# Two-layer hybrid transformer on one core: four conditioning chunks placed right behind a branch, norm diagonals made ahead of it, and the last combine moved

## The chip, the cores and the metric

One Trainium2 chip, one of its cores. The metric is the device time of one launch in microseconds (us); lower is better. Everything runs in one program on one core: TensorE (PE) multiplies, VectorE (DVE) and ScalarE (ACT) do the elementwise work, SyncE (SP) issues nearly all loads, GpSimd (POOL) only gathers rows.

## The reference, cut to what matters

```python
def trunk_layer(x, xc, mod, mod_c, ...):
    sh1, sc1, g1, sh2, sc2, g2 = jnp.split(mod[:, None, :], 6, axis=-1)
    h = modulate(rms_norm(x, norm1), sh1, sc1)
    hc = modulate(rms_norm(xc, norm1), sh1c, sc1c)
    y, yc = token_mixer(h, hc, ...)          # attention, Fourier, pooling branches
    x = x + g1 * y
    x = x + g2 * moe_ffn(modulate(rms_norm(x, norm2), sh2, sc2), ...)
    ...
for l in range(DEPTH):                       # DEPTH = 2
    mod = jax.nn.silu(c) @ w_ada[l] + b_ada[l]        # six vectors of 1024
    mod_c = jax.nn.silu(c_ctx) @ w_ada[l] + b_ada[l]
    x, xc = trunk_layer(x, xc, mod, mod_c, ...)
return rms_norm(x, norm_f)
```

256 tokens of x and 256 context tokens, width 1024, float32. `moe_ffn` sends each token to 2 of 16 experts (1024 to 512 to 1024). In layer 2 the context is needed only as keys and values, so the mixer's outputs and the experts work on the 256 tokens of x alone.

## The kernel before, in words

The tokens stay in SBUF as four tiles of 128 rows, two in X0 and two in X1. All weights are streamed from memory once, in chunks of mostly 1 MB. `Stream` (L172 and on) holds a list of chunks in the order in which the code asks for them with `W.get`. `fill` (L187) starts the next load on SP's queue (L219) as soon as the ring it belongs to has a free buffer: the `stage` ring has four buffers, and during the experts there are seven more (`ext`) and X1. A chunk of conditioning weights (`w_ada`) is used by PE as it is, in float32, and its buffer is free when PE has read it. Every other chunk is first split (`split`, L317) by ACT into a float16 high part (`whi`, L319) and by DVE into a low part (`wlo`, L323), and each product is three float16 matmuls, high by high, high by low, low by high (`mm3`, L577, with its matmuls on L580 to L582). `W.tick` splits chunks a little ahead of their use.

Layer 1's experts end in a data-dependent branch (L1510, L1511): if more tokens than fit chose one expert, extra rounds run, else it is passed over, as here. Each engine's instructions behind the branch are scheduled apart from those ahead of it, and no instruction can be moved across it. Ahead of the branch `batch` (L1348) finishes layer 1's result and the reciprocal norms (`rstd`, L532; its last DVE operation is on L459). It also makes the stream of layer 2, `Wn`, and lets it fill the stage ring (`Wn.fill`), so four loads are on their way when the branch is reached.

Behind the branch layer 2 begins (`layer`, L585; `mixer`, L614). `norm_steps` (L543) makes four diagonal matrices from the reciprocal norms (DVE, L555), multiplies X by them (64 float32 matmul records, L568), which transposes and scales it, applies shift and scale on ACT (16 operations `h`, L572), and splits the result in DVE (`hH` L573, `hL` L574). Then come the products of K and V for all 512 tokens, with the weights of the first chunks of `w_in`, then Q, then attention with the Fourier branch between.

A conditioning vector is made by `ada(l, which)` (L462). For each of four chunks 8 float32 matmuls (16 records, L500) read the chunk with 32 columns of the stationary side each, four of them side by side; the sum is split into `adah` and `adal`, and a second small product (L477, L478) turns it. `SIDE1` holds the one vector of layer 2 that isn't made in layer 1, the shift before the experts, `ada(1, 3)`. It is taken step by step as filler work within layer 2's attention. It isn't needed before the second norm of layer 2.

Layer 2's experts end otherwise than layer 1's (`pe_all`). All results but those of the last two experts are gathered by POOL (`fetch`, L1399) into `yg`; `combine(t)` (L1404) adds the two rows of each token with their weights (ACT L1406, DVE L1407) and, where `gated`, multiplies by the gate and adds to X (DVE L1409, L1410). For expert 15, `hidden` (L1380) makes `sa` (ACT L1382, DVE L1383), and `down` multiplies it by w2 in float32 (`py`, L1312). `accumulate` (L1333) scatters and sums into `acc`, `add` puts that on X, and the last norm and the stores follow.

## Time and profile before

| what | us |
|---|---|
| runs | 1455.19, 1453.69, 1454.68 |
| median | 1454.68 |
| the profiled execution's own time | 1449.04 |
| its span in the trace | 1447.3 |
| PE busy | 1345.9 (93%) |
| DVE busy | 1118.3 (77%) |
| ACT busy | 952.8 (66%) |
| POOL busy | 16.5 (1%) |

The profile is of one execution, and times within it are counted from the start of its span. Its own time lies 1.7 us above the span and 5.64 us below the median of the runs. A view in order of time gives each instruction's start, its duration and, in brackets, how long its engine stood idle before it and what ended that. Rows with `xN` group N instructions that follow one another. The branch lies at 856 to 857 us, layer 2 behind it.

### The profile page before, as it was taken

The page shows a single profiled execution, that of the slowest core. Times are in us where ns is not written, and L with a number is a line of the kernel's source. Part 1 is how long each engine was busy: PE and PEld are TensorE (multiplying, and loading weights), DVE is VectorE, ACT ScalarE, POOL GpSimd, SP SyncE. Part 2 cuts the span into 40 slices and gives each one's busy share as a digit, 9 for nine tenths or more (in the row PEclk, how much of TensorE's full clock was granted, in tenths as well). Part 3 has the DMA queues.
Part 4 walks back from the last instruction along what each step waited for, and adds up shares of the span by engine and source line. Part 5 has one row for each costly group of instructions (what it writes and reads, how often), then busy time and mean ns, then how long its engine had stood idle before and what let it go on. Part 6 is the DMA issues. An engine that isn't in the chain of part 4 may idle for free. (4 is left out here: it accounts for less than half of the span.)

```text
span 1447.3 us, 33640 instructions
## 1 busy us (share of the span) xinstructions
PE 1345.9 (93%) x14151; PEld 923.4 (64%) x14151; DVE 1118.3 (77%) x2003; ACT 952.8 (66%) x1431; POOL 16.5 (1%) x16
## 2 busy tenths in 40 slices
PE   5999999999999998999999978899999989999994
PEld 3545445444444586777777746577788767777771
DVE  3888647786554557898988889878977888989995
ACT  3777535665433347889888656856855569899981
POOL 0000000000000000000000010000000000000010
PEclk9999999999999999999999999999999999999997
DMA  9559772678794336789999564783999679999981
GB/s 365 216 132 222 217 232 88 175 219 228 238 364 159 131 101 250 293 344 420 395 419 380 222 253 163 200 240 103 238 310 364 239 280 342 420 420 418 405 327 63
DMA packets 146416, 383.31 MB, mean 265 GB/s; under 512 B 91856, under 2 KB 93904, under 8 KB 108112
## 3 DMA queue, kind: packets, MB, share of 16 engines
q1 hardware_dynamic: 133136, 355.24, 69.5%
q10 hardware_dynamic: 11392, 19.56, 3.6%
q0 software_dynamic: 1728, 6.29, 1.3%
q8 instruction: 112, 1.84, 0.5%
q14 instruction: 48, 0.39, 0.1%
HBM read 344.88 MB, written 15.20 MB: 249 GB/s over the span
## 5 line engine op out<-in xcount | busy, mean ns | idle before, releaser
L323 DVE SCALAR_TENSOR_TENSOR wlo<-stage,whi 128x1024 f16<-128x1024 f32 (+1 forms) x212 | 318.5, 1522 | 104.0 <-ACT whi L319 103.6
L582 PE MATMUL mm<-hH,wlo 128*128 128x96 f16 (+2 forms) x1824 | 395.5, 260 | 1.0 <-DVE wlo L323 1.0
L580 PE MATMUL mm<-hH,whi 128*128 128x96 f16 (+2 forms) x1824 | 395.3, 260 | 0.7 <-DVE gate L992 0.7
L581 PE MATMUL mm<-hL,whi 128*128 128x96 f16 (+2 forms) x1824 | 395.3, 260 | 0.0
L319 ACT ACTIVATE whi<-stage 128x1024 f16<-128x1024 f32 (+1 forms) x212 | 269.6, 1294 | 126.3 <-PE mm L581 86.7
L582 PEld LDWEIGHTS <-wlo 128*128 128x128 f16 x3104 | 304.0, 98 | 72.7 <-DVE wlo L323 2.7
L580 PEld LDWEIGHTS <-whi 128*128 128x128 f16 x3104 | 303.9, 98 | 71.6 <-issue 3.4
L581 PEld LDWEIGHTS <-whi 128*128 128x128 f16 x3104 | 303.9, 98 | 71.2 <-issue 1.2
L323 DVE SCALAR_TENSOR_TENSOR wlo<-ext,whi 128x2048 f16<-128x2048 f32 x116 | 262.1, 2286 | 42.6 <-ACT whi L319 42.6
L319 ACT ACTIVATE whi<-ext 128x2048 f16<-128x2048 f32 x116 | 217.8, 1904 | 9.4 <-PE mm L582 7.4
L581 PE MATMUL mm<-xg,whi 128*128 128x96 f16 x1024 | 132.3, 206 | 0.0
L582 PE MATMUL mm<-xg,wlo 128*128 128x96 f16 x1024 | 132.3, 206 | 0.0
L580 PE MATMUL mm<-xg,whi 128*128 128x96 f16 x1024 | 132.3, 206 | 0.0
L581 PE MATMUL py<-wlo,hd 128*96 128x512 f16 x240 | 90.9, 379 | 8.9 <-DVE wlo L323 8.7
L582 PE MATMUL py<-whi,hd 128*96 128x512 f16 x240 | 90.2, 381 | 6.8 <-DVE hd L321 6.0
L580 PE MATMUL py<-whi,hd 128*96 128x512 f16 x240 | 91.0, 379 | 0.0
L580 PE MATMUL mm<-brH,whi 128*128 128x512 f16 (+1 forms) x256 | 83.5, 326 | 0.0
L582 PE MATMUL mm<-brH,wlo 128*128 128x512 f16 (+1 forms) x256 | 83.4, 326 | 0.0
L581 PE MATMUL mm<-brL,whi 128*128 128x512 f16 (+1 forms) x256 | 83.4, 326 | 0.0
L1264 PE MATMUL mm<-Dg,merged 128*128 128x384 f16 x384 | 71.0, 338 | 3.8 <-DVE Dg L1197 1.8
L500 PE MATMUL mm<-stage,cpad 128*32 128x256 f32 x768 | 58.1, 406 | 13.3 <-DMA stage<-in_w_ada_dram 13.2
L825 DVE SCALAR_TENSOR_TENSOR P<-E,rl,P 128x512 f16<-128x512 f32 (+1 forms) x96 | 59.2, 658 | 9.7 <-ACT P L824 9.5
(313 smaller groups left out, 2050.3 us busy)
## 6 DMA issues: line engine op xcount, KB each, us to landing
ext<-in_w_dram SPq DMA_DIRECT2D x118, 1024.0 KB, 9.0
stage<-in_w_dram SPq DMA_DIRECT2D x62, 1024.0 KB, 9.0
stage<-in_w_ada_dram SPq DMA_DIRECT2D x48, 1024.0 KB, 6.3
stage<-in_w_gate_dram SPq DMA_DIRECT2D x32, 1024.0 KB, 5.8
stage<-in_w_in_dram SPq DMA_DIRECT2D x16, 1024.0 KB, 6.9
stage<-in_w_branch_dram SPq DMA_DIRECT2D x32, 512.0 KB, 4.6
ydram<-ys ACTq DMA_DIRECT2D x56, 192.0 KB, 7.1
stage<-in_w_out_dram SPq DMA_DIRECT2D x8, 1024.0 KB, 5.5
```

The costliest lines, as they stand in the source:

```text
L319: a = nc.scalar.activation(hi, src, AF.Copy, scale=scale)
L323: b = nc.vector.scalar_tensor_tensor(lo, src, scale, hi, op0=ALU.mult, op1=ALU.subtract)
L500: pe.matmul(ps[32 * j:32 * j + 32, :], self.cpad[:, 2 * k:2 * k + 32], st[:, k, :], start=k < 4, stop=k >= 4, tile_position=(0, 32 * j))
L580: pe.matmul(ps, wH(k), xH(k), start=first and k == 0, stop=False)
L581: pe.matmul(ps, wH(k), xL(k), start=False, stop=False)
L582: pe.matmul(ps, wL(k), xH(k), start=False, stop=last and k == nk - 1)
L825: dve.scalar_tensor_tensor(pv[:, 1, qt, :], E[qt][:, 0:nk], r[:, qt:qt + 1], pv[:, 0, qt, :], op0=ALU.mult, op1=ALU.subtract)
L1264: pe.matmul(ps[:, 0:SLOTS], h2[n][t][:, cs(k)], Dg[:, t].rearrange("p e c -> p (e c)"), start=t == 0, stop=t == ntt - 1)
```

## The change

`ada(1, 3)` leaves the filler work. Its first products, for all four chunks, stand right behind the branch (`ada_sums`), into a PSUM tile of their own name (`adas`); the rest of it (`adah`, `adal`, second products) runs after `norm_mod`. So the four chunks that are loaded ahead of the branch are now chunks of `w_ada`, and the first chunks of `w_in` are loaded behind it, each when PE has read one of the four. The four diagonals of layer 2's first norm are made in `batch`, ahead of the branch, in a buffer of their own. `combine(0, True)` of the last layer moves behind `hidden(15)`, and the DVE operations of `hidden(15)` and of the gated `combine` keep the order of the program. The area for POOL's DMA descriptors is set to 8192.

```diff
-SIDE1 = ((1, 3),)
...
+        self.diag = const.tile([128, 4, 128], F32, "diag1")
...
+    def ada_sums(self, l, which):
+
+        W, out = self.W, []
+        for c in range(4):
+            st = W.get("ada", "w_ada", (l,), which * D + c * 256)
+            if c % 2 == 0:
+                bank = self.ps.tile([128, 512], F32, "adas", tag="pst")
+            ps = bank[:, c % 2 * 256:c % 2 * 256 + 256]
+            self.ada_products(ps, st)
+            out.append(ps)
+        return out
...
         for c in range(4):
-            st = W.get("ada", "w_ada", (l,), which * D + c * 256)
-            ps = self.mm((128, 256))
...
+            if sums:
+                ps = sums[c]
+            else:
+                st = W.get("ada", "w_ada", (l,), which * D + c * 256)
+                ps = self.mm((128, 256))
+                self.ada_products(ps, st)
+                if tick:
+                    W.tick()
...
-        dg = wk.tile([128, 4, 128], F32, "diag", tag="t2")
-        for t in range(ntt):
-            dve.tensor_scalar(dg[:, t, :], self.C("ident"), r[:, t:t + 1], None, op0=ALU.mult)
+        if l and n == 1:
+            dg = self.diag
+        else:
...
         else:
             self.W = self.Wn
-            side = chain(*(self.ada(*x) for x in SIDE1))
+            first = self.ada(l, 3, False, self.ada_sums(l, 3))
+            side = None
...
         hH, hL = self.h if full else self.norm_mod(l, 1, NTOK, 0, 2)
+        if first:
+            run_all(first)
...
                         if t >= 2:
                             self.rstd(self.rnorm, (0, 3)[t - 2], t + 1, 2)
+                            for u in range((0, 3)[t - 2], t + 1):
+                                dve.tensor_scalar(self.diag[:, u, :], C("ident"), self.rnorm[:, u:u + 1], None, op0=ALU.mult)
...
-                dve.scalar_tensor_tensor(sa, pb, AS * DS, sa, op0=ALU.mult, op1=ALU.mult)
+                last = dve.scalar_tensor_tensor(sa, pb, AS * DS, sa, op0=ALU.mult, op1=ALU.mult)
+                if pe_all and e == NE - 1:
+                    tc.keep_in_program_order(last)
...
-                dve.scalar_tensor_tensor(y0, y1, wr[:, 1, t:t + 1], y0, op0=ALU.mult, op1=ALU.add)
+                both = dve.scalar_tensor_tensor(y0, y1, wr[:, 1, t:t + 1], y0, op0=ALU.mult, op1=ALU.add)
                 if gated:
+                    tc.keep_in_program_order(both)
...
-                if e == NE - 1 and pe_all:
-                    combine(0, True)
...
                 prev = hidden(e, pa, pb)
                 if e == NE - 1 and pe_all:
+                    combine(0, True)
                     combine(1, True)
...
-    nc = _bacc.Bacc("TRN2", target_bir_lowering=False, num_devices=1)
+    nc = _bacc.Bacc("TRN2", target_bir_lowering=False, num_devices=1, dynamic_dma_scratch_size=8192)
```

The scheduler decides most of the order, so the diff doesn't show where the instructions come to stand. Line numbers of the changed kernel differ (L318 for `whi`, L477 for the conditioning products, L593 for `h`, L601 to L603 for `mm3`, L1434 for ACT's part of `combine`).

**ACT behind the branch**, before:

```order
L319 ACTIVATE whi<-stage 128x1024 x2
L654 DMA turns<-in_staged_dram 128x512
L572 ACTIVATE h_16333<-mm,ada_1_3703,ada_1_2550 128x256 x2
L319 ACTIVATE whi<-stage 128x1024
L572 ACTIVATE h_16343<-mm,ada_1_3703,ada_1_2550 128x256 x2
...
L572 ACTIVATE h_16403<-mm,ada_1_3703,ada_1_2550 128x256 x2
L319 ACTIVATE whi<-stage 128x1024 x2
L388 DMA tabs<-in_staged_dram 128x512
L388 DMA tabs<-in_staged_dram 128x260
L388 DMA tabs<-in_staged_dram 128x130
L319 ACTIVATE whi<-stage 128x1024
```

And in the changed kernel:

```order
L678 DMA turns<-in_staged_dram 128x512
L593 ACTIVATE h_16377<-mm,ada_1_3704,ada_1_2551 128x256 x2
L318 ACTIVATE whi<-stage 128x1024 x2
L593 ACTIVATE h_16387<-mm,ada_1_3704,ada_1_2551 128x256 x2
...
L593 ACTIVATE h_16447<-mm,ada_1_3704,ada_1_2551 128x256 x2
L318 ACTIVATE adah<-adas 128x256
L318 ACTIVATE whi<-stage 128x1024 x2
L318 ACTIVATE adah<-adas 128x256
L318 ACTIVATE whi<-stage 128x1024 x2
L318 ACTIVATE adah<-adas 128x256 x2
L388 DMA tabs<-in_staged_dram 128x512
...
L318 ACTIVATE dftth<-tabs 128x512
```

Of the first six `whi` (three chunks of `w_in`) two stood ahead of all `h` and one behind the first two. Now none stands ahead of the first `h`, two stand behind the first two, and the other four, with the three first `adah`, behind all sixteen.

**PE behind the branch**, before (`X0`, `X1` are the token tiles):

```order
L1511 UNCONDITIONAL_BRANCH
L1569 BRANCH_PREFETCH_HINT
L568 MATMUL mm_16328<-diag_16317,X0_4729 128x128 x2
L568 MATMUL mm_16328<-diag_16317,X1_4730 128x128 x2
...
L568 MATMUL mm_16398<-diag_16317,X0_4729 128x128 x2
L568 MATMUL mm_16398<-diag_16317,X1_4730 128x128 x2
L580 LDWEIGHTS whi_16322
L580 MATMUL mm_16433<-hH_16315,whi_16322 128x512
L581 LDWEIGHTS whi_16322
L581 MATMUL mm_16433<-hL_16316,whi_16322 128x512
```

And in the changed kernel (`adas` the sums of the conditioning products, `x8` the 8 matmuls of a chunk):

```order
L1597 BRANCH_PREFETCH_HINT
L477 MATMUL adas_16321<-stage_11248,cpad_99 32x256 x8
L477 MATMUL adas_16321<-stage_11251,cpad_99 32x256 x8
L477 MATMUL adas_16342<-stage_11254,cpad_99 32x256 x8
L477 MATMUL adas_16342<-stage_11257,cpad_99 32x256 x8
L589 MATMUL mm_16372<-diag1_97,X0_4730 128x128 x2
...
L589 MATMUL mm_16442<-diag1_97,X1_4731 128x128 x2
L495 LDWEIGHTS adah_16453
L495 MATMUL mm_16457<-sel16_104,adah_16453 128x2
L496 LDWEIGHTS adal_16454
...
L601 LDWEIGHTS whi_16366
L601 MATMUL mm_16524<-hH_16364,whi_16366 128x512
```

The conditioning products of four chunks stand ahead of the norm's products, and the second products of three chunks, with the first of the fourth, between these and the first product of K (L580, now L601). On SP's queue, five chunks of `w_in` now follow the branch, then one of the expert weights (into X1) and the gates; before, it was a chunk of `w_ada`, the one into X1, a chunk of `w_in` and three more of `w_ada`.

**ACT at the end of layer 2**, before (`whi<-X` is the high part of expert 15's w3 chunk in X1):

```order
L1382 ACTIVATE sa<-mm 128x384
L319 ACTIVATE whi<-ext 128x2048
L319 ACTIVATE yHL<-py,slotw 96x512
L319 ACTIVATE whi<-X_24636 128x2048
L319 ACTIVATE yHL<-py,slotw 96x512
L1406 ACTIVATE yg<-yg,wr 128x1024 x2
L1296 COPY hotT<-hotT 96x256
```

And in the changed kernel:

```order
L1408 ACTIVATE sa<-mm 128x384
L318 ACTIVATE whi<-ext 128x2048
L318 ACTIVATE yHL<-py,slotw 96x512
L1434 ACTIVATE yg<-yg,wr 128x1024
L318 ACTIVATE whi<-X_24638 128x2048
L318 ACTIVATE yHL<-py,slotw 96x512
L1434 ACTIVATE yg<-yg,wr 128x1024
L1320 COPY hotT<-hotT 96x256
```

The first weighted row of `combine(0)` now stands ahead of the high part of the chunk in X1. On DVE, `sa` of expert 15 (L1383) stood behind both `combine`s' weighted sums (L1407) and one L1409; now it stands ahead of them all.

## Rows read from the trace of the kernel before

**Rows 1.** The page's first section: busy us, share of the span, instructions.

```profile
PE 1345.9 (93%) x14151; PEld 923.4 (64%) x14151; DVE 1118.3 (77%) x2003; ACT 952.8 (66%) x1431; POOL 16.5 (1%) x16
```

**Rows 2.** Tile view of the stage buffers, 843 to 845.5: first and last issue; landing, us.

```profile
L219 SPq DMA_DIRECT2D stage<-in_w_in_dram x4: 328/350/576, 843.4 to 844.9; - x4
...
DMA to landing us min/median/max: 4.8/9.1/12.1
```

**Rows 3.** Timeline of DVE, 855 to 859: start us, duration us, instruction, [idle before <-releaser].

```profile
855.75 0.16 DVE L459 SCALAR_TENSOR_TENSOR rnorm<-rs_t,rs_y 128x1 f32<-128x1 f32 x1
...
857.96 0.88 DVE L555 TENSOR_SCALAR diag<-cst,rnorm 128x128 f32<-128x128 f32 x4
```

**Rows 4.** Timeline of PE, 858 to 868, same columns.

```profile
858.40 9.53 PE L568 MATMUL mm<-diag,X 128*128 128x128 f32 x64 [7.56 <-DVE diag L555]
867.76 0.38 PE L580 MATMUL mm<-hH,whi 128*128 128x512 f16 x1
```

**Rows 5.** Groups by line on ACT, 857 to 880: busy us, mean ns, idle before.

```profile
L319 ACT ACTIVATE whi<-stage 128x1024 f16<-128x1024 f32 x8 | 8.2, 1067 | 4.5 <-DVEq L1511 3.8 <-DVE tabs L387 0.7
L572 ACT ACTIVATE h<-mm,ada,ada 128x256 f32<-128x256 f32 x16 | 7.6, 581 | 1.5 <-PE mm L568 1.4
```

**Rows 6.** Stretches behind the branch: us, busy us by engine, granted clock, DMA share, GB/s.

```profile
862.00:864.00 2.00, 2.00 (x16) 2.00 (x16) 1.97 (x4) 1.87 (x4) 0.00 (x0) 0.78 0.97 262
864.00:868.00 4.00, 4.00 (x38) 3.87 (x37) 3.85 (x9) 4.00 (x10) 0.00 (x0) 1.00 0.31 131
```

**Rows 7.** Timeline of PE: conditioning products at the start, and within layer 2's attention.

```profile
16.09 1.94 PE L500 MATMUL mm<-stage,cpad 128*32 128x256 f32 x16 [1.50 <-DMA stage<-in_w_ada_dram]
...
901.70 1.07 PE L500 MATMUL mm<-stage,cpad 128*32 128x256 f32 x16
```

**Rows 8.** DMA view, issues within 861 to 861.6.

```profile
stage<-in_w_ada_dram SPq DMA_DIRECT2D x1, 1024.0 KB, 4.7
```

**Rows 9.** Tile view of adah, 890 to 945: durations ns min/median/max, first and last start.

```profile
L319 ACT ACTIVATE adah<-mm x4: 377/393/397, 903.7 to 930.9; 128x256 f16<-128x256 f32 x4
```

**Rows 10.** Waits of PE, 880 to 945: us in total, times, longest.

```profile
PE po L840 <- DMA pt<-P: 4.6, 4, 2.1
PE pq L675 <- ACT sqh L319: 2.4, 2, 1.6
PE mm L717 <- DVE rk L704: 1.3, 1, 1.3
PE S L792 <- ACT E L811: 0.8, 3, 0.4
```

**Rows 11.** Stretches in and behind the attention.

```profile
924.00:928.00 4.00, 4.00 (x32) 1.33 (x31) 2.97 (x6) 3.09 (x9) 0.00 (x0) 0.57 0.80 181
945.00:995.00 50.00, 50.00 (x501) 42.27 (x499) 34.37 (x61) 26.86 (x41) 0.00 (x0) 1.00 0.63 192
```

**Rows 12.** Timeline of ACT near the end, 1406 to 1411.

```profile
1406.16 1.90 ACT L319 ACTIVATE whi<-X 128x2048 f16<-128x2048 f32 x1
...
1409.83 1.15 ACT L1406 ACTIVATE yg<-yg,wr 128x1024 f32<-128x1024 f32 x1 [0.85 <-DMA yg<-ydram,late]
```

**Rows 13.** Timeline of DVE near the end, 1408 to 1420.

```profile
1408.44 2.28 DVE L323 SCALAR_TENSOR_TENSOR wlo<-X,whi 128x2048 f16<-128x2048 f32 x1
...
1417.37 1.28 DVE L1407 SCALAR_TENSOR_TENSOR yg<-yg,wr 128x1024 f32<-128x1024 f32 x1 [1.84 <-DMA yg<-ydram,late]
...
1419.70 0.55 DVE L1383 SCALAR_TENSOR_TENSOR sa<-mm,sa 128x384 f32<-128x384 f32 x1
```

**Rows 14.** Timeline of PE near the end, 1413 to 1430.

```profile
1413.98 0.29 PE L1294 MATMUL hotT<-id,Dg 128*96 128x128 f16 x2
1420.31 8.25 PE L1312 MATMUL py<-stage,sa 128*96 128x512 f32 x12 [6.04 <-DVE sa L1383]
```

**Rows 15.** Stretches near the end.

```profile
1420.00:1422.00 2.00, 1.69 (x2) 0.68 (x3) 2.00 (x3) 0.00 (x0) 0.00 (x0) 0.50 0.00 0
```

**Rows 16.** Timeline of POOL near the end: the four gathers.

```profile
1408.98 2.55 POOL L1399 DMA_INDIRECT yg<-ydram,late  x1 [0.30 <-ACT yHL L319]
```

More of the change, by code (lines that the diff above doesn't have):

```diff
@@ L459, in rsqrt, with ada_products, ada @@
             dve.scalar_tensor_tensor(dst if it == 2 else y, t, 1.5, y, op0=ALU.add, op1=ALU.mult)
-    def ada(self, l, which, tick=True):
+    def ada_sums(self, l, which):
[8 more added lines that the diff above has]
+        return out
+    def ada_products(self, ps, st):
+        for k in range(KD):
+            j = k % 4
+            self.nc.tensor.matmul(ps[32 * j:32 * j + 32, :], self.cpad[:, 2 * k:2 * k + 32], st[:, k, :], start=k < 4, stop=k >= 4,
+                                  tile_position=(0, 32 * j))
+    def ada(self, l, which, tick=True, sums=None):
         nc, const, W = self.nc, self.const, self.W
@@ L610, in layer, with mixer @@
             self.late = self.ada(l, 5, False)
[L611 removed]
+            self.mixer(l, nq, side, None if full else first)
             self.moe(l, nq, side)
[L614 removed]
+    def mixer(self, l, nq, side, first=None):
         nc, tc, A, W, wk, sm = self.nc, self.tc, self.A, self.W, self.wk, self.sm
```

13 lines of the change are left out of this document (4 added, 9 removed).

## Prediction

> **What bounds the kernel now.** The page's first section comes first: PE is busy for 93% of the span [rows 1], so time is won or lost where PE waits. The change touches three such places: the branch between the layers, layer 2's attention, and the kernel's end.
>
> At the branch, the timeline of PE shows a wait of 7.56 us before the norm's products, and 9.36 us from their start to the first product of K [rows 4]. The branch itself waits for two things at once. DVE's last operation of the norm starts at 855.75 [rows 3]. The last of the four loads that stand ahead of it is issued at 844.9 and takes 12.1 us at most, so it lands by 857.0 [rows 2]. The engines go on at about 857.2, DVE makes the diagonals at 857.96 [rows 3], and PE starts at 858.40. Here the reader should note what ACT does in the time in which PE waits and transposes: it already splits `w_in`, which landed ahead of the branch.
>
> In the attention, the waits of PE from 880 to 945 add up to 9.1 us in the four largest groups, the longest of them for the DMA that transposes the probabilities [rows 10]. From 945 on PE is busy without a gap [rows 11], and the instructions stand in the old order from about there to the experts' last stage. So a delay in the head can be made up before 945 or not at all.
>
> At the end, PE stands idle for 6.04 us before `py`, until DVE has made `sa` at 1419.70 [rows 13, 14]. `sa` is late because it stands in DVE's queue behind `combine`'s sums, and the second of these waits for a gather until 1417.37 [rows 13].
>
> **The change, part by part.**
>
> *Diagonals ahead of the branch.* Four DVE operations took 0.88 us together [rows 3]. Three of them and the last one now stand in the chain that ends at 855.9, which then ends at 856.8 at the latest. That is inside the 857.0 of the landing, so I put it at nothing; if the chunk landed earlier it would cost up to 0.9. Behind the branch PE no longer waits for them and starts at about 857.5 instead of 858.40.
>
> *Conditioning products.* 64 records now stand ahead of the norm. Sixteen took 1.94 us where PE's clock was at its lower level and 1.07 at the upper [rows 7], 0.121 and 0.067 each. PE's granted clock is 0.78 in the mean of 862 to 864 and 1.00 after [rows 6]: half speed for 0.9 us of the two, so it rose at about 862.9, 4.5 us after PE's first product. From 857.5 that is 862.0. By then 37 records are done; the other 27 take 1.8 us, so they end at 863.8. The norm's products run behind them, eight records to the first `h`. All 64 took 9.53 us over both levels [rows 4]; at the upper level, twice the pace of the lower, I take 0.11 each, so the first `h` can start at about 865.0 with the hand-over to ACT.
>
> The Trainium skill says of the clock (TensorE: Matmul & The Clock Gate, section "The HAM clock gate") that the default state is throttled and activity releases it. By that rule the conditioning products serve as the activity, and the 863.8 holds; the rows agree for the norm's products, but show no rise during conditioning products of a quarter of the array's columns each.
>
> *Loads of `w_in`.* Each now waits until PE has read one conditioning chunk. The first is read after 1.94 us, at 859.4, and is issued at about 859.7; a lone load of 1 MB here took 4.7 us [rows 8], so it lands at 864.4. The others follow 1 to 2 us apart. On SP's queue the load into X1 and the gates wait behind these five, but nothing reads them before the attention.
>
> *ACT, the new bound of the head.* Before, two `whi` stood ahead of the first `h` in ACT's idle time. Now the queue holds all in one chain between 865.0 and K: 16 `h`, 7.6 us busy [rows 5]; six `whi` at 8.2 / 8 = 1.03 us [rows 5], 6.2 us; three `adah` at 0.39 [rows 9], 1.2 us. That is 15.0 us, to 880.0. PE's order then has the small products of chunk 2, which also need DVE's `adal`, ahead of K: 0.4 more. K starts at 880.4 instead of 867.76: **+12.6 us**. Nothing covers it: K's products are next in PE's queue, in order.
>
> *Given back in the attention.* Four groups of sixteen conditioning records at 1.07 us leave it [rows 7]: 4.3 us. The least it can give back is the clock's dip around 924 to 928, where the granted clock is 0.57, so 4 times 0.43 or 1.7 us [rows 11], if the other waits simply move along. The most is that, the products and all four groups of waits: 1.7 + 4.3 + 9.1 = 15.1 us. I take **-4.3**: the products are taken out of PE's line, but the waits come from DMA, ACT and DVE chains that keep their length, and the three `wlo` that the new order of loads brings earlier now stand in DVE's queue ahead of the attention's first work.
>
> *The end.* `sa` no longer waits for the gathers. But on ACT `combine(0)`'s first row, which waits for a gather until 1409.83 and takes 1.15 us [rows 12], now stands ahead of the `whi` of X1, which ran at 1406.16 before [rows 12]. So this `whi` (1.90) ends at about 1412.9, `wlo` (2.28 [rows 13]) at 1415.2, and PE ends the products that need it about 3.2 us on, at 1418.4, where `sa` is ready. `py` starts at 1418.4 instead of 1420.31: -1.9. Twelve records of `py` took 8.25 us [rows 14], most of them at a granted clock of 0.50 [rows 15], because PE had been idle since 1414 [rows 14]. If the clock now stays up, 12 records at about 0.43, half of the 0.86 that the lower level gives, take 5.2, up to 3.1 less. Of this I take 2.0, since DVE's sums now stand between `py` and the output. Together **-3.9**, with bounds of 0 (the late `whi` costs what `sa` gains) and -5.
>
> *POOL's area of 8192.* A gather took 2.55 us [rows 16] and POOL is busy for 1% of the span [rows 1]. Nothing; were the area too small for two gathers at a time, at most one gather's 2.5 us would show at the end.
>
> *Sum.* 12.6 - 4.3 - 3.9 = **+4.4 us** on the profiled execution's 1449.04, so 1453.4. The median of the runs stands 5.64 above that execution, so I forecast 1454.68 + 4.4 = **1459.1 us**.
>
> **The rivals.**
>
> *The attention takes it all up (faster).* The place is 880 to 945. If the conditioning products were what kept PE, ACT and DVE there from feeding each other, taking them away closes the waits too: 15.1 us back, 12.6 - 15.1 - 3.9 = -6.4, so 1448.3. It decides from 8.7 us given back on. For it: PE idles 9.1 us there [rows 10]. Against it: half of these waits are for DMA transposes, which no conditioning product delays. The Trainium skill's rule to relieve the engine with the highest occupancy first (Perfetto Trace Analysis, section "Identifying the Most-Contended Engine") points this way, as PE's products move to where PE stood idle; the idle time of 7.56 us, however, ends ahead of where they can start.
>
> *No change.* Some 8.7 us are given back, the products and half of the waits: 12.6 - 8.7 - 3.9 = 0, so 1454.7.
>
> *The clock stays low (slower still).* If the conditioning products, a quarter of the columns each, don't raise the clock, all 64 take 7.75 us, to 865.3, and the norm's first eight 1.7: K starts 2.4 us later, at 882.8. If it falls at the end as well, there remain -1.9 of the -3.9. 15.0 - 4.3 - 1.9 = +8.8, so 1463.5.
>
> *The change doesn't do what it says.* The order shows the products behind the branch and the diagonals ahead of it, so this can only be a branch that DVE ends instead of the landing: +0.9, inside the others.
>
> **How the numbers follow.** Chances: the forecast 0.52, the low clock 0.11, no change 0.22, faster 0.15. A measurement of this kernel can tell about 0.2% from no change, 2.9 us. The first two make slower, 0.63. The range: above, the low clock's 1463.5 with only the dip given back and -1.9 kept, 15.0 - 1.7 - 1.9 = +11.4, so 1466; below, 12.1 us given back and -4.1 at the end, 12.6 - 12.1 - 4.1 = -3.6, so 1451. That leaves most of the faster case out, and little above.
>
> **What would show it.** Right: in the timeline of PE, the conditioning products start near 857.5 and K's first product comes near 880, with ACT's idle time before K close to none; the waits in the attention stay for the transposes; `py` starts 1 to 3 us earlier relative to the gathers. Wrong: K's products start before 875, or the stretch up to PE's gapless part is no longer than before, or the granted clock behind the branch stays at 0.50 up to the norm's end.

## The result, and the profile after

The changed kernel takes 1463.83 us (median of 7 runs, 1458.73 to 1465.06); the kernel before, beside it, 1453.69 (7 runs). The ratio is 1.0066, 95% interval 1.0045 to 1.0087: slower by 9.6 us, where +4.4 was forecast. The direction and the range held. The sum did not: two of its terms were too large and the third had the wrong sign. The profiled execution took 1460.34 with a span of 1458.5, 11.2 more than before's 1447.3.

PE's busy time grew by 5.4 us for the same 14151 instructions [rows 1]. The page, its first section:

```profile
PE 1351.3 (93%) x14151; PEld 925.9 (63%) x14151; DVE 1119.0 (77%) x2003; ACT 953.5 (65%) x1431; POOL 15.1 (1%) x16
```

**How the losses are placed.** Ahead of the branch, where the edits do nothing, an execution already stands up to 4.2 us from that of before (0.46 us for the changed kernel, -0.95 in e2, 4.21 in e7). So I match PE's instructions one to one with before's and state how much later each starts, less the shift of PE's instruction at 840.35. For the changed kernel: K's first product **+9.1**, the stretch behind K's first products **+10.5**, Q's last small product **+13.7**, 975 to 1005 **+13.7**, the experts' end **+13.6**, the seventh of the twelve products `py` (before at 1425.5) **+10.4**; at the span's end it is 11.2 - 0.46 = 10.7. So there are three places: a loss in the head, a further one before the attention's scores, and a gain at the end.

**The head.** Timeline of PE behind the branch (start us, duration us, instruction, [idle before <-releaser]):

```profile
854.25 2.80 PE L477 MATMUL adas<-stage,cpad 128*32 128x256 f32 x48 [2.95 <-ACTq L1539]
857.90 1.07 PE L477 MATMUL adas<-stage,cpad 128*32 128x256 f32 x16 [0.85 <-SPq L1539]
858.90 4.73 PE L589 MATMUL mm<-diag,X 128*128 128x128 f32 x40
866.02 4.57 PE L589 MATMUL mm<-diag,X 128*128 128x128 f32 x24 [2.38 <-ACT h L593]
872.03 0.18 PE L495 MATMUL mm<-sel,adah 128*128 128x2 f16 x1 [1.44 <-ACT adah L318]
...
877.34 0.59 PE L601 MATMUL mm<-hH,whi 128*128 128x512 f16 x1
...
878.57 0.63 PE L601 MATMUL mm<-hH,whi 128*128 128x512 f16 x1
...
880.62 0.38 PE L601 MATMUL mm<-hH,whi 128*128 128x512 f16 x1
```

PE does not start at 857.5 but at 854.25. The engines do not pass the branch together: PE is behind it and at work while DVE, ahead of it, still makes the last diagonal. Timeline of DVE:

```profile
856.93 0.29 DVE L1393 TENSOR_SCALAR diag<-cst,rnorm 128x128 f32<-128x128 f32 x1
```

Forty-eight records are done by 857.05, the last chunk's sixteen follow at 857.90, when it has landed, and the norm's products start at 858.90, where before they started at 858.40 [rows 4]. Then PE waits for ACT. Timeline of ACT:

```profile
860.16 1.02 ACT L593 ACTIVATE h<-mm,ada,ada 128x256 f32<-128x256 f32 x2 [6.31 <-PE mm L589]
863.06 2.00 ACT L318 ACTIVATE whi<-stage 128x1024 f16<-128x1024 f32 x2 [1.88 <-DMA stage<-in_w_in_dram]
864.97 6.73 ACT L593 ACTIVATE h<-mm,ada,ada 128x256 f32<-128x256 f32 x14
...
871.86 2.00 ACT L318 ACTIVATE whi<-stage 128x1024 f16<-128x1024 f32 x2
...
874.01 2.01 ACT L318 ACTIVATE whi<-stage 128x1024 f16<-128x1024 f32 x2
875.90 0.39 ACT L318 ACTIVATE adah<-adas 128x256 f16<-128x256 f32 x1
```

This is the forecast chain of 16 `h`, six `whi` and the `adah`, in the forecast order. It starts 5 us earlier than I had it (860.16), stands 1.88 us for the first chunk of `w_in` (the `whi` that waits for it starts at 863.06; the landing was forecast for 864.4), goes on without a gap, and ends at 876.3. K's first product starts at 877.34 instead of the forecast 880.4. But the first products of K then run at half pace: from 877.34 a product every 0.43 us, from 880.6 one every 0.215. The stretches, with the granted clock as the last number but two:

```profile
858.00:862.00 4.00, 4.00 (x43) 3.42 (x44) 0.88 (x5) 1.02 (x2) 0.00 (x0) 1.00 0.67 229
866.00:872.00 6.00, 4.57 (x24) 4.38 (x24) 5.93 (x13) 5.95 (x14) 0.00 (x0) 0.72 1.02 426
878.00:880.00 2.00, 2.00 (x9) 0.75 (x8) 1.59 (x7) 0.00 (x0) 0.00 (x0) 0.51 0.97 393
915.00:920.00 5.00, 4.74 (x28) 3.40 (x29) 4.74 (x20) 1.86 (x6) 0.00 (x0) 0.50 0.35 138
```

The clock is at its upper level (2.4 GHz, 1.00) through the conditioning products and the norm's first 40 records. It had not fallen ahead of them: PE stood idle for 2.95 us there, and before, where it stood for 7.56, the clock is 0.50 from 858 to 862. It falls after PE has stood 2.38 us for `h` (0.72 in 866 to 872), and from 872 on PE has only small products, most with a wait ahead. K therefore meets the lower level (1.2 GHz, 0.51 in 878 to 880, and 1.00 again in 880 to 882), which adds 1.3 us. Before, K's first product came straight behind the norm's at full pace.

**The attention.** `S` are the scores, `E` their exponentials, `P` the probabilities, `pt` the transposed probabilities and `po` their products with V; `sqh` and `sql` are the high and low part of Q's squares, and `f` and `G` belong to the Fourier branch. Waits of PE, 890 to 960 (us in total, times, longest):

```profile
PE pq L699 <- ACT sqh L318: 5.6, 2, 4.9
PE po L864 <- DMA pt<-P: 1.5, 1, 1.5
```

Against [rows 10] the transposes cost less (2.8 by 975 instead of 4.6), but the wait for `sqh` grew from 1.6 to 4.9 at its longest, and a wait for `G` is new (2.0 us). Timelines of ACT and of DVE (the first and the last of three `wlo`) ahead of the `sqh`:

```profile
904.75 1.99 ACT L318 ACTIVATE whi<-stage 128x1024 f16<-128x1024 f32 x2
...
910.26 1.05 ACT L318 ACTIVATE whi<-stage 128x1024 f16<-128x1024 f32 x1
...
914.71 0.42 ACT L318 ACTIVATE sqh<-sq 128x256 f16<-128x256 f32 x1
```

```profile
908.23 1.23 DVE L322 SCALAR_TENSOR_TENSOR wlo<-stage,whi 128x1024 f16<-128x1024 f32 x1
...
911.85 1.22 DVE L322 SCALAR_TENSOR_TENSOR wlo<-stage,whi 128x1024 f16<-128x1024 f32 x1
```

Three `whi` and three `wlo` of the next chunks (gates and branch weights) stand in the chain that makes Q's squares. Before, the stream had four conditioning chunks in these places of the order, and those are not split at all. Taking them out moved the splits forward. PE stands for 4.87 us, and the clock falls to 0.50 in 915 to 920.

The transposes' own queue then keeps about its length. Tile view of `pt`, first before, then the changed kernel (first and last issue before the semicolon):

```profile
L772 SPq DMA_TRANSPOSE pt<-P x8: 1961/3110/4703, 913.2 to 951.1; - x8
```

```profile
L796 SPq DMA_TRANSPOSE pt<-P x8: 1317/2436/4937, 928.0 to 967.3; - x8
```

From the first to the last issue it is 37.9 and 39.3 us, and from the first issue to the last landing 46.2 in both. In the changed kernel PE waits for the last transpose, which lands at 974.2:

```profile
974.27 0.38 PE L864 MATMUL po<-pt,vH 128*64 128x256 f16 x3 [1.26 <-DMA pt<-P]
```

Before, it had landed at 959.4, and PE came to these products at 960.1 without a gap. With less to do, PE had made up some of its delay (13.7 us at `sqh`, 10.9 at 945 and 12.2 just ahead of this wait), but behind the wait it is 13.7 again: what PE had less to do did not bring the transposes forward.

**The end.** Timelines of ACT, DVE and PE:

```profile
1423.83 1.15 ACT L1434 ACTIVATE yg<-yg,wr 128x1024 f32<-128x1024 f32 x1 [3.54 <-DMA yg<-ydram,late]
1424.89 1.89 ACT L318 ACTIVATE whi<-X 128x2048 f16<-128x2048 f32 x1
```

```profile
1432.78 0.56 DVE L1409 SCALAR_TENSOR_TENSOR sa<-mm,sa 128x384 f32<-128x384 f32 x1 [3.02 <-PE mm L603]
```

```profile
1433.80 5.34 PE L1336 MATMUL py<-stage,sa 128*96 128x512 f32 x12
```

As forecast, the `whi` of X1 stands behind ACT's weighted row, `sa` no longer stands behind the gathers, and `py` follows it at full pace: 5.34 us for the twelve records instead of 8.25 [rows 14].

### The profile page after: what moved, and what is told of

Same layout as the page of the kernel before. It is cut to its first block, busy times and chain, and to the rows that moved or that the text cites. A ratio compares the mean times of both kernels' runs of the same rounds, so it can differ in the third digit from the quotient of the medians.

```text
span 1458.5 us, 33654 instructions
## 1 busy us (share of the span) xinstructions
PE 1351.3 (93%) x14151; PEld 925.9 (63%) x14151; DVE 1119.0 (77%) x2003; ACT 953.5 (65%) x1431; POOL 15.1 (1%) x16
## 5 line engine op out<-in xcount | busy, mean ns | idle before, releaser
L601 PE MATMUL mm<-hH,whi 128*128 128x96 f16 (+2 forms) x1824 | 398.5, 261 | 3.2 <-ACT whi L318 2.5
L603 PE MATMUL mm<-hH,wlo 128*128 128x96 f16 (+2 forms) x1824 | 398.5, 261 | 2.4 <-DVE wlo L322 2.2
L603 PEld LDWEIGHTS <-wlo 128*128 128x128 f16 x3104 | 304.9, 98 | 75.4 <-DVE wlo L322 4.4
L601 PEld LDWEIGHTS <-whi 128*128 128x128 f16 x3104 | 304.8, 98 | 75.3 <-issue 4.8
L318 ACT ACTIVATE whi<-stage 128x1024 f16<-128x1024 f32 (+1 forms) x212 | 269.1, 1292 | 118.2 <-PE mm L602 86.6
L318 ACT ACTIVATE whi<-ext 128x2048 f16<-128x2048 f32 x116 | 217.9, 1904 | 9.3 <-PE mm L603 7.4
L601 PE MATMUL mm<-xg,whi 128*128 128x96 f16 x1024 | 132.4, 206 | 0.4 <-issue 0.4
L603 PE MATMUL mm<-xg,wlo 128*128 128x96 f16 x1024 | 132.4, 206 | 0.0
L603 PE MATMUL py<-whi,hd 128*96 128x512 f16 x240 | 90.2, 381 | 6.8 <-DVE hd L320 6.0
L601 PE MATMUL py<-whi,hd 128*96 128x512 f16 x240 | 91.0, 379 | 0.0
L601 PE MATMUL mm<-brH,whi 128*128 128x512 f16 (+1 forms) x256 | 83.5, 326 | 0.0
L603 PE MATMUL mm<-brH,wlo 128*128 128x512 f16 (+1 forms) x256 | 83.4, 326 | 0.0
L477 PE MATMUL mm<-stage,cpad 128*32 128x256 f32 x704 | 53.8, 408 | 14.1 <-DMA stage<-in_w_ada_dram 14.0
L821 DVE TENSOR_REDUCE mx<-S 128x1 f32<-128x512 f32 (+1 forms) x96 | 56.4, 595 | 13.5 <-PE S L820 13.2
```

Source lines behind the costliest of these rows:

```text
L318: a = nc.scalar.activation(hi, src, AF.Copy, scale=scale)
L477: self.nc.tensor.matmul(ps[32 * j:32 * j + 32, :], self.cpad[:, 2 * k:2 * k + 32], st[:, k, :], start=k < 4, stop=k >= 4, tile_position=(0 ...
L601: pe.matmul(ps, wH(k), xH(k), start=first and k == 0, stop=False)
L603: pe.matmul(ps, wL(k), xH(k), start=False, stop=last and k == nk - 1)
L821: dve.tensor_reduce(mx[:, qt:qt + 1], S, axis=AX.X, op=ALU.max)
```

## The experiments

The table gives the ratio to the kernel before on the same chip, and how many us later than before PE starts the same instruction, less the shift at 840.35 (one profiled execution each; e11's layer 1 lies ahead of 840 and is told apart). "Q" is where Q's products begin (before at 891.9), "sqh" the small product that waits for the last `sqh` (before at 901.0), "960" the products just ahead of the last transpose's `po`, and "`py`" the seventh of its twelve records (before at 1425.5).

| kernel | ratio (95%) | K first | Q | sqh | 960 | 995 | experts' end | `py` |
|---|---|---|---|---|---|---|---|---|
| changed | 1.0066 (1.0045 to 1.0087) | 9.1 | 10.5 | 13.7 | 12.2 | 13.7 | 13.6 | 10.4 |
| e1 end only | 0.9981 (0.9966 to 0.9997) | 0.1 | 0.1 | 0.1 | 0.0 | 0.0 | -2.5 | -5.7 |
| e2 diagonals only | 0.9983 (0.9965 to 1.0001) | 0.0 | 0.1 | 0.1 | 0.3 | 0.3 | -2.2 | -2.4 |
| e3 both of these | 0.9974 (0.9961 to 0.9987) | -0.5 | -0.5 | -0.5 | 0.0 | 0.0 | -0.3 | -3.3 |
| e4 conditioning only | 1.0081 (1.0064 to 1.0098) | 9.0 | 10.9 | 14.2 | 12.9 | 14.1 | 14.3 | 14.1 |
| e5 second products later | 1.0036 (1.0019 to 1.0053) | 2.1 | 8.7 | 11.9 | 8.4 | 9.3 | 7.7 | 4.4 |
| e6 splits held back | 1.0062 (1.0040 to 1.0083) | 9.3 | 11.0 | 11.0 | 9.5 | 14.0 | 14.2 | 11.3 |
| e7 three chunks | 1.0070 (1.0046 to 1.0093) | 3.7 | 6.3 | 9.5 | 7.6 | 9.3 | 7.4 | 4.2 |
| e8 two chunks | 1.0022 (1.0008 to 1.0035) | 1.7 | 3.4 | 6.7 | 7.5 | 7.5 | 7.4 | 4.5 |
| e9 products doubled | 1.0020 (1.0005 to 1.0035) | -0.2 | -0.1 | -0.1 | 2.9 | 2.9 | 3.3 | 0.6 |
| e10 more at the end | 0.9940 (0.9916 to 0.9964) | -0.1 | -0.1 | -0.1 | 0.2 | 0.2 | 1.1 | -7.8 |
| e11 chunks in layer 1 | 1.0039 (1.0021 to 1.0057) | -0.3 | 0.1 | 3.3 | 2.1 | 2.4 | 0.3 | -2.8 |
| e12 one product a chunk | 0.9992 (0.9977 to 1.0007) | -0.2 | -0.2 | -0.2 | -0.5 | -0.5 | -3.0 | -5.9 |

Near 1000 every execution waits 2.5 us for an `E`. Behind that wait the granted clock falls to 0.50 in six of them (before, changed, e3, e4, e6, e8) and stays at 1.00 in the other eight, which so gain about 1.7 us. That goes with the execution, not with the edit (up to there e1 is the kernel before), so I read each term within one profile, on either side of its place.

### e1: the end alone

```diff
-                if e == NE - 1 and pe_all:
-                    combine(0, True)
...
                 if e == NE - 1 and pe_all:
+                    combine(0, True)
                     combine(1, True)
```

with the two `keep_in_program_order` of the change.

> The kernel before with only the end changed: combine(0) behind hidden(15), and the order of the program kept for sa and the gated sums. Theory (the end is a gain by itself): py starts about 2 us earlier and runs at the upper clock, so the span is 3 to 4 us shorter than before, everything ahead of 1406 us unchanged. Rival (the high part of the X1 chunk, now behind a gather, costs what sa gains): span within 1 us of before.

Measured: 0.9981, the medians 3.5 us apart (1448.15 and 1451.61). From the experts' end to `py` PE gains 3.2 us. Timeline of PE:

```profile
1418.85 5.34 PE L1312 MATMUL py<-stage,sa 128*96 128x512 f32 x12
```

The same 5.34 us as in the changed kernel. The term of the end, forecast at -3.9, is -3.2 here and in the changed kernel.

### e2 and e3: the diagonals alone, and with the end

```diff
+            if l and n == 1:
+                dg = self.diag
...
+                            for u in range((0, 3)[t - 2], t + 1):
+                                dve.tensor_scalar(self.diag[:, u, :], C("ident"), self.rnorm[:, u:u + 1], None, op0=ALU.mult)
```

> The kernel before with only the diagonals made ahead of the branch, in a buffer of their own, and the descriptor area of 8192. Theory (no cost of its own): PE starts the norm's products 1 to 2 us earlier, and K's first product comes 0.5 to 1.5 us earlier; span 0 to 1.5 us shorter. Rival 1 (ACT sets when K starts, whatever PE does): K's first product within 0.3 us of before, span the same. Rival 2 (the smaller descriptor area slows the gathers): span 1 to 3 us longer, and the gathers at the end last longer than 2.6 us.

> The change without its conditioning part: diagonals ahead, end changed, ada(1,3) left as filler work in the attention. Theory (head and attention lose by the conditioning chunks alone): span 3.5 to 5 us shorter than before, so 14 to 16 us shorter than the changed kernel. Rival (diagonals or descriptor area cause part of the loss): span less than 2 us shorter than before, or longer.

Timeline of PE in e2, and a stretch:

```profile
856.92 10.09 PE L572 MATMUL mm<-diag,X 128*128 128x128 f32 x64 [7.03 <-DVEq L1517]
```

```profile
862.00:864.00 2.00, 2.00 (x17) 2.00 (x17) 1.44 (x4) 1.48 (x3) 0.00 (x0) 0.85 0.95 385
```

The norm's products start 0.5 us earlier against the shift at 840, yet K's first does not (+0.04): the diagonals cost nothing and bring nothing. K comes when rival 1 has it, but not for its reason: the products run without a gap in both kernels, so it isn't ACT that holds them. The clock is still at 0.50 up to 862 (0.85 in 862 to 864, before 0.78 [rows 6]), so an earlier start only lets more of the 64 records run at the lower level: 26 of them 0.21 us apart, before 20, and the rest 0.11 apart. The four gathers at the end take 0.94 to 2.55 us, as before, which leaves nothing for rival 2. The ratio of e2 can't be told from 1; e3 (0.9974) is e1's gain within its interval.

### e4: the conditioning chunks alone

The changed kernel with the diagonals and the end of before.

```diff
-            side = chain(*(self.ada(*x) for x in SIDE1))
+            first = self.ada(l, 3, False, self.ada_sums(l, 3))
+            side = None
```

> The kernel before with only the conditioning chunks moved behind the branch. Theory: the whole loss of head and attention, about 11 and 3 us, without the end's gain: span 13 to 16 us longer than before (about 1 per cent). Diagonals are made behind the branch again, but PE has the conditioning products to do in that time, so they cost nothing here. Rival (the diagonals ahead of the branch are part of the loss): span less than 11 us longer than before.

Measured: 1.0081, 11.8 us, between the rival's 11 and the 13 to 16 expected; PE at `py` is 14.1 us late. The losses in the head (K's first product at 877.79) and ahead of the scores are those of the changed kernel, without its gain at the end. With e3's -0.0026 the two parts make 1.0055, against 1.0066 for the whole: within the intervals the parts add up.

In this execution the clock had fallen ahead of the conditioning products, and it rose while they ran (from 854.80 to 859.85). Stretches:

```profile
856.00:858.00 2.00, 2.00 (x28) 0.96 (x24) 0.79 (x5) 0.00 (x0) 0.00 (x0) 0.58 0.06 25
858.00:860.00 2.00, 2.00 (x38) 1.01 (x31) 0.97 (x7) 0.00 (x0) 0.00 (x0) 1.00 0.39 70
```

### e5: the second products later

```diff
         hH, hL = self.h if full else self.norm_mod(l, 1, NTOK, 0, 2)
-        if first:
-            run_all(first)
...
+            if first and glob:
+                run_all(first)
```

so that `adah`, `adal` and the second products stand behind K's products.

> The changed kernel with the rest of ada(1,3) (its adah, adal and second products) put behind the products of K and V instead of ahead of them; the four chunks' first products stay right behind the branch. Theory (PE's order chains K behind adah and adal, and these stand behind four whi in ACT's queue): K's first product comes at about 873 instead of 877.3, limited by the last h and hL, PE's clock does not fall ahead of K, and the span is 3 to 6 us shorter than the changed kernel's. Rival (the sum of ACT's and DVE's work sets the pace, whatever the order): the work comes back within the products of Q, and the span is less than 1.5 us shorter.

Timeline and waits of PE:

```profile
871.99 0.38 PE L601 MATMUL mm<-hH,whi 128*128 128x512 f16 x1
```

```profile
PE mm L496 <- DVE adal L322: 2.4, 2, 1.3
PE mm L495 <- ACT adah L318: 1.8, 3, 1.0
```

K's first product comes 7 us earlier than in the changed kernel and at full pace: PE's order, with the second products ahead of K, was what held K back. But the waits move with them. They now stand ahead of Q (4.2 us of waits, with the clock at 0.55 in 885 to 890), and PE loses 6.6 us from K to Q, where the changed kernel loses 1.4. What is left of the 7 us is 1.8 at `sqh` and 4.4 at 995; the ratio is lower by 0.0030, also 4.4 us, though the two intervals overlap.

### e6: the early splits held back

The splits of the first gate and branch chunks are held until Q's projections are done, and kept in program order, so that no `whi` or `wlo` of theirs stands in Q's chain. Four of their loads come as in the changed kernel; the next two wait for buffers that the splits free, and come at 941.5 and 942.9 instead of 911.3 and 913.1.

```diff
+            if self.hold and self.order[j][1] in ("w_gate", "w_branch"):
+                return
...
+        pin = self.hold_pin > 0 and spec[1] in ("w_gate", "w_branch")
...
+            W.hold = glob and not full
```

> The changed kernel with the splits of the first gate and branch chunks held back until the projections of Q are done (the order of the program is kept for these three). Theory (these splits, which the new order of the stream pulls forward, delay the last sqh): PE's longest wait for sqh falls from 4.9 us to 1.5 to 2.2, the granted clock stays at 1.00 from 910 to 920, and the span is 3 to 6 us shorter than the changed kernel's. Rival (the splits are needed soon after, so their wait only moves): PE waits for wlo or the gates instead, and the span is within 1.5 us of the changed kernel's.

Waits of PE, 890 to 960 and then 960 to 1000, and stretches:

```profile
PE pq L711 <- ACT sqh L327: 2.4, 2, 1.7
```

```profile
PE po L877 <- DMA pt<-P: 3.4, 2, 2.6
```

```profile
915.00:920.00 5.00, 4.46 (x59) 3.51 (x60) 4.75 (x20) 2.50 (x7) 0.00 (x0) 1.00 0.00 0
...
975.00:980.00 5.00, 4.07 (x33) 3.36 (x33) 0.42 (x1) 0.38 (x1) 0.00 (x0) 0.66 0.99 361
```

The wait for `sqh` is back to before's 2.4 and the clock stays up, so the splits are what made it: at `sqh` and at 960 PE is 2.7 us ahead of the changed kernel. Behind 960 all of it is lost: PE waits for the transposes (3.4 us in 960 to 1000 of its own trace) and then meets the lower clock, and at 995 it is 0.3 us behind. The transposes there land late. DMA view, 955 to 985:

```profile
pt<-P SPq DMA_TRANSPOSE x4, 7.9
```

7.9 us in the median, where the changed kernel's longest is 6.9. Loads run beside the transposes in both kernels, so why they take longer here is not shown. The time is the changed kernel's (1.0062). So holding the splits back gains nothing: the transposes bind instead.

### e7 and e8: three chunks, two chunks

```diff
-        for c in range(4):
+        for c in range(2):
...
-            first = self.ada(l, 3, False, self.ada_sums(l, 3))
-            side = None
+            first = side = self.ada(l, 3, True, self.ada_sums(l, 3))
```

(3 in e7); the other chunks stay filler work of the attention.

> The changed kernel with three of the four conditioning chunks behind the branch, and the fourth as filler work in the attention; so the first chunk of w_in is loaded ahead of the branch again. Theory (what delays K is that the first chunk of w_in lands late, and the conditioning work in ACT's and PE's queues ahead of K): K's first product comes at about 871, 6 us earlier than in the changed kernel, since two whi run ahead of the first h again; span 5 to 9 us shorter than the changed kernel's. Rival (each conditioning chunk costs its share): K's first product at about 875, a quarter of the head's loss given back; span 2 to 3.5 us shorter.

> The changed kernel with two conditioning chunks behind the branch and two as filler work. Theory: K's first product at about 869, with only one adah ahead of it on PE; the end's gain stays, so the span is 1 to 4 us shorter than the kernel before. Rival (each chunk its share): K's first product at 872 to 873, span 1 to 3 us longer than the kernel before.

Timeline of PE in e8:

```profile
872.12 0.18 PE L495 MATMUL mm<-sel,adah 128*128 128x2 f16 x1 [2.76 <-ACT adah L318]
```

With two chunks K is only 1.7 us late, 3.4 with the clock, which falls after 2.76 us of waiting for an `adah`; with three 3.7 and 6.3. So the head's loss grows with the chunks that stand ahead of `w_in`. The `sqh` wait costs the same 3.3 us in both, and e8 is still slower by 3.2 us: of two, three and four chunks none pays. K comes near the time that the two theories gave it, but the gain that they forecast is not there. In e7 the profiled execution, the fastest of its runs, is 4.2 us behind before at `py`, while the ratio says 10 us. I leave its time open.

### e9: the products doubled

On e3, the 64 conditioning records in the attention are made twice. The second pass begins the sums anew, so the vector keeps its values.

```diff
-            for k in range(KD):
+            for k in list(range(KD)) * (2 if (l, which) == (1, 3) else 1):
```

> The kernel of e3 (diagonals ahead, end changed, ada(1,3) as filler work in the attention) with the conditioning products of these four chunks issued twice into the same PSUM tile, so that PE does 4.3 us more within the attention. Theory (the attention's length is set by the chain of eight transposes of the probabilities, which takes 44 to 47 us in every run so far, and PE's filler work lies beside it): first issue to last landing of the transposes stays within 44 to 47.5 us, PE reaches the stretch behind the attention less than 1.5 us later than in e3, and the span is within 2 us of e3's. Rival (PE's work bounds the attention, which is what the prediction's term of 4.3 us given back rests on): everything behind the attention comes 3.5 to 5 us later.

Tile view of `pt`, and waits of PE 890 to 960:

```profile
L776 SPq DMA_TRANSPOSE pt<-P x8: 1817/3230/3797, 914.8 to 951.3; - x8
```

```profile
PE po L844 <- DMA pt<-P: 3.3, 2, 2.2
```

The transposes are issued over 36.5 us, no longer than before's 37.9, and from the first issue to the last landing take 42.0, less than the 44 to 47.5 expected. But PE reaches the stretch behind the attention 2.9 us later, and is 3.9 later at `py`; the ratio is 0.0046 (6.7 us) above e3's. So 4.3 us more on PE are not hidden: the wait for the transposes takes up 1.6 of them (4.9 us in e3, 3.3 here). The last transpose has landed at 956.8, and PE comes to its products at 964.3, 7.5 us later (in e3 1.6). So there PE's own line sets the end when its work grows, as the rival has it; e12 is the other half.

### e10: more at the end

On e3, the Silu of expert 15's `sa` is also kept in program order and the load of the last norm's weights stands behind `combine`, so that ACT's `whi` of X1 comes ahead of the weighted rows again.

```diff
-                act.activation(sa, pa, AF.Silu, scale=DS)
+                silu = act.activation(sa, pa, AF.Silu, scale=DS)
+                if pe_all and e == NE - 1:
+                    tc.keep_in_program_order(silu)
```

> The kernel of e3 with ACT's part of combine(0) kept behind the high part of the chunk in X1 (the order of the program is kept for the Silu of expert 15, and the load of the last norm's gain is issued behind combine). Theory (in the changed end the whi of X1 waits behind a gather, and PE's last up products with it): the products with the low part come about 4 us earlier, py starts 3 to 4.5 us earlier relative to 1400 us than in e3, and the span is 2 to 4 us shorter than e3's. Rival (the second gather and DVE's sums set the end anyway): span within 1 us of e3's.

Timelines of ACT, DVE and PE:

```profile
1408.09 1.90 ACT L319 ACTIVATE whi<-X 128x2048 f16<-128x2048 f32 x1
...
1411.70 1.15 ACT L1416 ACTIVATE yg<-yg,wr 128x1024 f32<-128x1024 f32 x1 [0.42 <-DMA yg<-ydram,late]
```

```profile
1415.01 0.56 DVE L1391 SCALAR_TENSOR_TENSOR sa<-mm,sa 128x384 f32<-128x384 f32 x1 [1.69 <-issue]
```

```profile
1416.04 5.34 PE L1316 MATMUL py<-stage,sa 128*96 128x512 f32 x12
```

ACT's order is `whi`, then the row, against the row, then `whi`, in the changed kernel. Up to 1389 PE is 0.6 us ahead of before; then the granted clock is 0.50 in 1390 to 1392, where e3 has 1.00, and at the experts' end PE is 1.1 behind. At `py` it is 7.8 ahead, so 8.9 are gained at the end, against 3.0 in e3; the ratio is 0.0034 below e3's, 4.9 us, where 2 to 4 were expected. The time is 1442.89 us, 0.9940 of before (0.9916 to 0.9964): the best of all these kernels, and faster than both that were compared.

### e11: the chunks in layer 1

On e3, `ada(1, 3)` is made with the other vectors of layer 2 in layer 1, so that neither the head nor the attention has it.

```diff
-SIDE0 = ((0, 2), (0, 4), (0, 3), (1, 1), (1, 0), (1, 2), (1, 4))
-SIDE1 = ((1, 3),)
+SIDE0 = ((0, 2), (0, 4), (0, 3), (1, 1), (1, 0), (1, 2), (1, 4), (1, 3))
+SIDE1 = ()
```

> The kernel of e3 with ada(1,3) made as the last filler work of layer 1 instead of within layer 2's attention, so that the head of layer 2 is as before and its attention has no conditioning work, as in the changed kernel. Theory (taking the conditioning chunks out of the stream pulls three splits ahead into the chain of Q, and the attention gives nothing back): K starts as in e3 relative to the branch, the last sqh comes 3 to 3.5 us later, and the first transposes are issued and the last landed 2.5 to 4 us later than in e3. Rival (the prediction's term): the stretch behind the attention comes 3 to 5 us earlier than in e3. What layer 1 pays for the four chunks, 0 to 5 us, is read apart, ahead of the branch.

Waits of PE, 890 to 960:

```profile
PE pq L679 <- ACT sqh L319: 5.6, 2, 4.9
```

The head is that of before, and the wait for `sqh` is that of the changed kernel, to a tenth (5.6, longest 4.9). It comes from the four chunks' absence in the attention's stream, wherever they went. Behind the attention PE is 2.4 us later than in e3 and before, with 4.3 us less to do: 0.9 of the 3.3 came back, no more. In layer 1 the four chunks cost 4.7 us, about 1.2 at each, as PE runs there without a wait. This lies ahead of 840 and is not in the table; it is half of the 9.4 us by which the ratio is above e3's.

### e12: one product a chunk

On e3, the chunks stay where they are, but each is read by one full-width product instead of eight narrow ones: 8 records for 64. A product with the identity takes the place of the sums, so this kernel leaves out what makes the vector's values.

```diff
+            if (l, which) == (1, 3): pe.matmul(ps, self.C("ident"), st[:, 0, :], start=True, stop=True)
-            for k in range(KD):
+            for k in range(KD) if (l, which) != (1, 3) else ():
```

> On e3 (diagonals ahead and the end), each of the four conditioning chunks of layer 2's attention is read by one float32 matmul of 256 columns instead of eight of a quarter of the stationary columns; the loads, the splits and the small second products stay. One of layer 2's vectors is then made from an eighth of its sum. About 64 records fall to 8 or 16, some 3.5 of their 4.3 us leave PE's line, and nothing moves ahead in the stream. Theory (in the attention PE and the chain from scores to transposes end together, so less work on PE alone brings nothing): the wait of PE for the transposes grows from 4.9 to 7 or more, PE reaches 960 to 1005 at most 0.8 us earlier than in e3, the transposes are issued over 37 to 39 us as in e3, and the ratio is e3's, 0.996 to 0.999. Rival (PE's line sets the attention's length, and the changed kernel lost the 4.3 us only to the wait for sqh and the lower clock): PE is 2.5 to 3.5 us earlier at 960 to 1005, and the ratio is about 0.995.

Stretch 900 to 945, first e3, then e12, and the tile view of `pt` in e12:

```profile
900.00:945.00 45.00, 36.82 (x403) 23.49 (x401) 38.79 (x111) 35.00 (x77) 0.00 (x0) 0.96 0.68 174
```

```profile
900.00:945.00 45.00, 36.63 (x352) 24.84 (x349) 40.48 (x115) 35.93 (x80) 0.00 (x0) 0.92 0.71 184
```

```profile
L776 SPq DMA_TRANSPOSE pt<-P x8: 1923/3958/5542, 914.7 to 953.0; - x8
```

Some 50 records fewer stand in the stretch, and PE is busy as long (36.6 us against 36.8), since the granted clock falls from 0.96 to 0.92. The edit takes less off PE than was meant: the products of a chunk take 0.65 to 0.70 us instead of 1.07, so some 1.6 us leave its line, not 3.5. The transposes are issued over 38.3 us, as in e3. PE reaches 960 to 995 0.5 us earlier than in e3, and the time does not go below e3's (0.9992). The wait for the transposes did not grow to 7 as expected (4.7): the freed time went into the lower clock and a wait for `f` (0.8 us instead of 0.2). So with nothing else moved, taking products out of the attention brings 0.5 of 1.6 us. More was hardly to be had: the last transpose lands at 960.7, and PE comes to its products at 961.3 (in e3 at 961.0 and 962.6). Before, PE and the chain from scores to transposes end within 0.7 us of each other: more work on PE shows (e9), less does not for long.

## Why the prediction was right or wrong

- *Diagonals ahead: 0.* Right (e2). That PE would start at 857.5 was wrong: 854.25, since the branch lets each engine through by itself. The 3 us were of no use, as PE then waited for ACT; and in e2, where PE doesn't wait, the lower clock takes up what the earlier start gives.
- *Conditioning products: end at 863.8.* Wrong by 5 us (858.9). I took the clock to be at its lower level behind the branch and to rise 4.5 us after PE's first product; it had not fallen (1.07 us for the last sixteen). So the rival in which the clock stays low over these products fell. In e4 the clock had fallen, and rose from 0.58 to 1.00 while they ran. The Trainium skill (TensorE: Matmul & The Clock Gate, section "The HAM clock gate") has it that activity releases the throttle; the trace of e4 agrees that these products are such activity.
- *ACT's chain to K: +12.6.* The mechanism is right and the size was off. The chain is the forecast one and nothing covers it, but it began 5 us earlier and then waited 1.9 for the first `w_in` (which came at 863.0 instead of 864.4): +9.1 to K's first product. What I left out is that PE, waiting, comes to K at the lower clock: 1.3 more. Together +10.5.
- *Given back in the attention: -4.3.* **This is the step that failed.** I took the products' 4.3 us out of PE's line and let the waits keep their length. Measured from behind K to 995 it is +3.3. The six splits that moved ahead stand in Q's chain and cost 3.2 at `sqh` (e11: the same 3.3 without any change in the head); I had named the three `wlo` among them and given them no price. And without that wait there is still little to get: in e12 some 1.6 us of products alone are taken out, and 0.5 us comes back. In the changed kernel the stretch ends with the transposes, whose issues still span 39 us: PE waits 1.26 us for the last of them. In e3, with nothing taken out, the last transpose lands 1.6 us before PE comes to it, so as long as the transposes stay where they are, 1.6 us is about the most that less work on PE could give there, not 4.3. My "least", 1.7 us of the clock's dip, was no lower bound either, since the clock fell elsewhere (915 to 920).
- *The end: -3.9.* Right: -3.2 in the changed kernel and e1, -3.0 in e3, by the forecast steps: full pace for `py`, and `whi` behind ACT's row eating part of it. e10 shows the price of the latter (with a load moved too): 4.9 us by the ratios, 5.9 within the profiles (8.9 against 3.0).
- *POOL's area: 0.* It was not tried apart. e2 and e3, which have it, show no loss, and e2's gathers take as long as before's.
- *The sum.* 10.5 + 3.3 - 3.2 = +10.6 from the trace (+10.4 at `py`), +9.6 in the runs. That this lies inside the range is luck in part: the range's upper end came from a low clock behind the branch, and what happened was a loss in the attention that the sum did not have. The rival that the attention takes it all up needed 8.7 us back; none came. For it the prediction drew on the Trainium skill's rule to work first on the engine with the highest occupancy (Perfetto Trace Analysis, section "Identifying the Most-Contended Engine"). The section judges TensorE not by its matmul share but by others, the share of its weight loads among them, and here these are busy for 64% and DVE for 77% [rows 1], so by that measure the rule does not point at PE.

What stays open: which part of the chain from scores to transposes (the maximum, `E`, `P` or the transposes themselves) sets its length. It was 46.2 us from the first issue to the last landing before, 45.7 in e3, and 42.0 in e9 with more work on PE; no run shortened it alone. And e7's time.

## What to carry to other kernels

Work that leaves an engine's line is only worth what the chain beside it lets through; where two chains end together, ask what each costs alone before counting either as given back, and price what moves into the freed places of the stream, as a chunk that needs no split hides splits behind it. Work put into an idle stretch is free only if its loads take no one's place: here four chunks put `w_in` behind themselves, and the splits that ACT had done in its idle time fell into the critical chain. And where an engine has been made to wait, look at its clock on the first products after the wait.

## What was unexpected of the hardware

- A branch taken by all engines is not a point where they meet: in the changed kernel PE's first product behind it starts at 854.25, while DVE's last operation ahead of it starts at 856.93, and SP's first load behind it is issued at 858.2.
- After a wait of 2.38 us, and of 2.76 in e8, with a few small products behind it, the granted clock was at 0.50 when the next large products came (changed kernel 878 to 880, e8 from 873). It cost 1.3 and 1.7 us, and 2.6 in e7.
- The same wait doesn't always do it. Near 1000 PE waits 2.47 us for an `E` before and 2.48 in e1, in the same code; behind it the clock is 0.50 in the one and 1.00 in the other. Stretch, first before, then e1:

```profile
1000.00:1002.00 2.00, 2.00 (x12) 1.39 (x11) 1.95 (x7) 0.33 (x1) 0.00 (x0) 0.50 0.81 262
```

```profile
1000.00:1002.00 2.00, 2.00 (x18) 1.49 (x17) 1.99 (x5) 1.78 (x6) 0.00 (x0) 1.00 0.24 31
```

- The start of a kernel differs between executions ahead of any edit, by -0.95 (e2) to 4.21 us (e7) against before at 840, more than some of the effects here. Single spans can't be compared; instructions placed against a common one can.
